# Mixing product of a decoder layer: the second and third block taken together with four seven-multiplication units, and one feed-forward block without sums prepared ahead

## The chip, the core and the metric

The kernel runs on one core of one Trainium2 chip. The metric is the device time of one execution in microseconds (us). Lower is better. The engines of the core have short names in the profile: PE is the matrix engine (PEld its weight loads), DVE the vector engine, ACT the scalar engine, POOL the general engine, and SP the engine that only issues DMA transfers here. Each engine works through its own queue in the order in which the program wrote it. L12 is line 12 of the kernel file.

## What is computed

The kernel computes one decoder layer on 256 tokens of width 2048, all in float32: a half feed-forward, a pair of token mixers (retention and sliding-window attention) with gates, a second half feed-forward, and a gated embedding, each followed by a residual addition and a layer norm. Only these lines matter here:

```python
mixed = (sigmoid(gate_r) * ret_branch + sigmoid(gate_a) * att_branch) @ w_mix_out   # 256x2048 @ 2048x2048
h = layer_norm(alpha * h + mixed, ln_g[1], ln_b[1])
g, u = split(h @ w_ffn2_gu)                                                         # 256x2048 @ 2048x11264
h = layer_norm(alpha * h + 0.5 * (silu(g) * u) @ w_ffn2_down, ln_g[2], ln_b[2])
```

The product with `w_mix_out` is called the mixing product below.

## The kernel before

**A product in three matmuls.** Every operand is kept as two parts, a rounded high part and the low part that is left. One float32 product of a 128x128 piece of the activations and a 128x512 piece of the weights is three matmuls (L393 low by high, L394 high by high, L395 high by low). For each 512 KB of weights, ACT makes the high part (L98) and DVE the low part by a subtraction (L99). `split` (L97) is the helper for both.

**Plain units.** A plain unit, `Single` (L133), is one weight chunk of 256 rows by 512 columns: 1 load, one 128x1024 copy on ACT, one 128x1024 subtraction on DVE, and 12 matmuls for the 256 tokens. A pair of plain units (kind P, with p the pair of row blocks) covers 1024 columns with 24 matmuls. A `Folded` unit (L147, the second of a pair of kind F) is a plain unit whose low part is made by ACT and an adding DMA issued by POOL (L164), with no work for DVE.

**Seven-multiplication units.** `Seven` (L166, kind S) does the work of a plain pair with seven block products instead of eight, so with 21 matmuls. For it DVE makes four sums of weight blocks (L189 to L192, each 128x512) and four low parts (three of 128x1024, one of 128x512), and ACT four high parts. On the activations' side it needs four combinations of blocks, the forms, which `forms_of` (L481) makes once for each group of 512 rows: `whole` adds the two parts (L478), `seven_forms` makes four sums (L466 to L469), and `split` parts the result; DVE waits for ACT's copy in between. `block` (L425) walks through a list of units. It sums the sevens' shared products into four banks of their own (p1, p6, p7, q5), and after the last seven `seven_common` (L497) combines these on DVE (L501 to L504). The eight banks of the accumulator memory are then all in use: four for the block's own sums and four for the sevens.

**Sums prepared ahead.** Kind D, `Prepared` (L209), is a seven unit whose sums and their parts were made much earlier by `sums_ahead` (L238), written to device memory, and are only read back. `AHEAD` (L43) names the blocks of the second feed-forward and the pairs that are treated so. `sums_ahead` is a generator that goes one step whenever `run_side` (L329) is called; the last two entries, those of block 7, are made during the mixing product (L1489).

**The order of the work.** The order on each engine is written out by hand. `plan` lists all units in the order of use. A small planner, `fill` (L279), runs each time a unit is done with: it makes the next loaded units until 45 matmuls' worth (`ahead`) is made in advance, and issues loads until 90 (`far`) is loaded or made, as long as the slots for weights allow it (16 in the mixing product, L1488). A plain unit keeps 2 slots and needs 1 to load and 2 to make; a seven keeps 7 and needs 2 to load and 6 to make. What the planner emits stands in the queues of SP, ACT and DVE at that place of the program, in front of all that is written later.

**The mixing product.** `mixers` (L1136) ends with it. Four blocks of 512 columns (mo0 to mo3) have 8 plain units each. The transposed activations `mix_t` come from `turned` (L1452), which runs as side work: its last four pieces run in the first block. For blocks 0 to 2 the residual block is loaded (L1494), the product is run (`tokens_out`, L405), and DVE adds it to the residual (L1497) and takes the statistics for the norm (L765). The load of the norm's vectors (`load_for_norm`, L775) stands ahead of block 2. In block 3 the last four units are held: `held_out` (L527) first finishes the first 128 tokens, then `Norm` (L652) combines them (L665, which calls L1485), takes the norm, and PE transposes the result (L644, tiles `lnps`) while the other 128 tokens are still computed. At the first unit of block 3 the planner is opened to 26 slots and 136 matmuls (L1504), so it then makes the rest of the mixing weights, two units of the small product `w_pp` and the first six units of the second feed-forward, all ahead of that combination in DVE's queue.

**The second feed-forward.** Eleven blocks of 512 gate and 512 up columns. `gu_units` (L873) gives each block's order: block 7 is PPSDSDSP, with three sevens and two prepared ones; block 8 is PPSSPSSP with four sevens. The first feed-forward has FFSSFSSF.

Of the kernel before, what the change touches and what calls it, by code (L numbers as in the profile page):

```python
# [12 lines left out]
ALU = mybir.AluOpType  # L13
# [9 lines left out]
ALPHA = 2.0**0.25  # L23
LN_EPS = 1e-5
GN_EPS = 1e-5
KD = D // P
# [13 lines left out]

SEVEN = (0, 1, 2, 3)

AHEAD = {1: (4, 5), 2: (4,), 3: (4, 5), 4: (4,), 5: (4, 5), 7: (4, 5)}  # L43
AHEAD_SLOTS = 32

SEVEN_DOWN = (6, 7, 8, 9)
# [9 lines left out]
def layer(ctx: ExitStack, tc: tile.TileContext, io):  # L56
# [348 lines left out]
    def tokens_out(key, n_k, lhs, ps, n=512, before=None):  # L405

        nk = 1024 // n
        sums = [Sum(ps[t][:, :n], n_k) for t in range(2)]
        for c in range(n_k // nk):
            u = take(key + (c,))  # L410
            tokens_chunk(u.chunk, c * nk, lhs, sums, (0, 1), range(nk))
            done(u)
            run_side()
# [11 lines left out]
    def block(name, units, keys, lhs, forms, sums, fold, before=None):  # L425


        sevens = [p for kind, p in units if kind in "SD"]
        if sevens:
            p1, p6, p7, q5 = (Sum(bank(f"{name}s{j}"), len(sevens)) for j in range(4))  # L430
        for j, (kind, p) in enumerate(units):
            if before is not None:
                before(j)
            if kind in "PF":
                for n in range(2):
                    u = take(keys(n, p))
                    tokens_chunk(u.chunk, 2 * p, lhs, [sums[t][n] for t in range(2)], (0, 1))
                    done(u)
                    run_side()
                continue  # L440
            u = take(keys(0, p))
            a11, a12 = (half_of(lhs(2 * p + e), 0) for e in range(2))
            a22 = half_of(lhs(2 * p + 1), 1)
            f5, f6, f7, f3 = forms(p)
            q2, q3, q4 = sums[0][0], sums[0][1], sums[1][0]
            steps = [
                (p1, a11, u.b11), (q2, a12, u.b21), (q3, f3, u.b22), (q5, f5, u.t1),
                (p7, f7, u.t3), (p6, f6, u.t2), (q4, a22, u.t4),
            ]
            if p == sevens[-1]:  # L450
                steps = [steps[j] for j in (0, 3, 5, 4, 1, 2, 6)]
            for to, left, right in steps:
                to.add(left, right)
            done(u)
            run_side()
            if p == sevens[-1]:
                fold(p1.ap, p6.ap, p7.ap, q5.ap)
# [415 lines left out]
    def gu_units(name, j):  # L873
        if j == 0:
            return [("P", p) for p in range(KD // 2)]
        if name == "f2" and j in AHEAD:
            return units_of(*(("PPSDSDSP", SEVEN[:3]) if j % 2 else ("PPSSDSSP", SEVEN)), AHEAD[j])
        order = "PPSSPSSP" if j % 2 == 0 else "PPSPSPSP"
        if name == "f1":
            order = "FFSSFSSF"  # L880
        return units_of(order, SEVEN[: order.count("S")])

# [220 lines left out]
    GATE_UNITS = units_of("PPSSPSSP", (0, 1, 2, 3))  # L1103
    RET_UNITS = units_of("PPPSPSPP", (0, 1))
    gate_keys = lambda b: lambda n, p: ("w_in_f2", 29 + 4 * b + 2 * n, p)
    ret_keys = lambda b: lambda n, p: ("w_ret2", 4 * b + 2 * n, p)

    def plan_mixers():
        plan_tokens(("w_rv", 0), KD)
        for grp in range(8):  # L1110
            plan_features([("w_in_f", grp)], KD)
        for blk in range(1, 4):
            plan_tokens(("w_rv", blk), KD)
        for grp in range(8, 16, 2):
            plan_tokens(("w_in_f2", grp), KD)
        plan_tokens(("w_av",), KD, nk=4)
        for grp in (20, 16, 17, 18, 19):
            plan_features([("w_in_f", grp)], KD)
        for grp in range(21, 29, 2):
            plan_tokens(("w_in_f2", grp), KD)  # L1120
        for b in range(2):
            block_units(GATE_UNITS, gate_keys(b))
        for j in range(0, 8, 2):
            plan_tokens(("w_att2", j), KD // 2)
        for b in range(2):
            block_units(RET_UNITS, ret_keys(b))
        for blk in range(4):
            plan_tokens(("w_mix", blk), KD)

    def later(n, job):  # L1130
        for j in range(n):
# [4 lines left out]
    def mixers(ht, norm, residual, keepers, away):  # L1136
# [291 lines left out]
                act.copy(sig[-1][:, t], ps[t])  # L1428
        assert not side

        def mixer_block(name, units, keys, lhs):

            ps = [banks(name + w) for w in "ab"]
            got = []
            block(name, units, keys, lhs, forms, block_sums(ps, units, KD), lambda *a: got.extend(seven_common(*a)))
            for n in range(2):
                for t in range(2):
                    dve.tensor_tensor(got[n][:, t], got[n][:, t], ps[t][n], ALU.add)
# [47 lines left out]

        lhs = lambda k: of_pairs(mix_t, k)
        slots_for_weights(16)  # L1488
        lazy.append(sums_ahead(ahead[8:], 3, 2))  # L1489
        for blk in range(3):  # L1490
            if blk == 2:
                load_for_norm(1)
            ps = banks(f"mo{blk}")
            y[blk] = load_columns(residual, blk, "mixy")  # L1494
            tokens_out(("w_mix", blk), KD, lhs, ps)
            for t in range(2):
                dve.scalar_tensor_tensor(y[blk][:, t], y[blk][:, t], ALPHA, ps[t], ALU.mult, ALU.add)  # L1497
            block_stats(stats, y, blk)
        y[3] = load_columns(residual, 3, "mixy")
        ps = banks("mo3")  # L1500
        sums = [[Sum(ps[t], KD)] for t in range(2)]
# [316 lines left out]
```

## Time and profile before

| | us |
|---|---|
| median of 3 runs | 2270.05 (2269.02 to 2270.55) |
| the profiled execution | 2269.44 |
| span of its instructions | 2267.3 |

The profile is of one execution. Its span is 2.1 us shorter than the execution's own time. The granted clock of PE was 0.999 over the span. A row of the timeline has the start in us from the span's beginning, the length in us, the engine, the line, the operation, what it writes and reads, the shape, the count of merged instructions, and in brackets the idle time of the engine before it with what ended it. A row of the windows view gives the busy time of each engine in one stretch, with the number of instructions in parentheses.

### The profile page before, as it was taken

What the parts mean: (1) busy time and instruction counts of PE and PEld (TensorE: products, weight loads), DVE (VectorE), ACT (ScalarE), POOL (GpSimd) and SP (SyncE); (2) the same over time, 40 slices, a digit from 0 to 9 for tenths busy, and PEclk for the clock granted to TensorE, in tenths of its full rate; (3) what the DMA queues carried; (4) which work ended last, traced back from release to release, by engine and by line L of the source; (5) the groups of instructions that cost most, each with busy time, mean ns of one, the idle gap of its engine ahead of it and who ended that gap; (6) DMA issues with size and microseconds to landing.
All of it is one profiled execution on the core that took longest, in us unless ns stands there. A gap on an engine that the chain in (4) does not pass through costs nothing.

```text
span 2267.3 us, 29270 instructions
## 1 busy us (share of the span) xinstructions
PE 2258.9 (100%) x10482; PEld 1877.7 (83%) x10482; DVE 1975.9 (87%) x2576; ACT 1272.5 (56%) x1543; POOL 37.1 (2%) x49
## 2 busy tenths in 40 slices
PE   9999999999999999999999999999999999999998
PEld 7888888888888888888778888888888888888887
DVE  7988989999989887888789788689999999889887
ACT  6676776656555444535566454455555565555543
POOL 0000010000000000000000000000000000000000
PEclk9999999999999999999999999999999999999999
DMA  9888898865677878775456568787867766555772
GB/s 316 249 261 252 238 262 243 250 208 186 216 285 261 291 282 289 256 236 183 140 158 225 183 211 293 271 288 247 297 242 250 255 197 218 196 190 209 290 269 73
DMA packets 216889, 536.69 MB, mean 237 GB/s; under 512 B 17052, under 2 KB 21532, under 8 KB 216744
## 3 DMA queue, kind: packets, MB, share of 16 engines
q1 hardware_dynamic: 209000, 511.28, 65.9%
q0 software_dynamic: 5760, 20.97, 5.1%
q10 hardware_dynamic: 1984, 2.58, 0.4%
q8 instruction: 82, 1.34, 0.2%
q14 instruction: 63, 0.52, 0.1%
HBM read 484.43 MB, written 29.36 MB: 227 GB/s over the span
## 4 chain that ended last, share of the span: by engine, by line
PE 78%; DVE 1%; DMA 1%; ACT 0%; issue 0%; ACTq 0%; DVEq 0%
PE f2g L395 3%; PE f2g L393 3%; PE f2g L394 3%; PE rqk L344 3%; PE f2u L393 2%; PE f2u L395 2%; PE f2u L394 2%; PE aqk L344 2%; PE f1d L395 2%; PE f2d L394 2%; PE f2d L395 2%; PE f1d L393 2%; PE f1d L394 2%; PE f2d L393 2%; PE f1e L395 1%; PE f2e L394 1%
## 5 line engine op out<-in xcount | busy, mean ns | idle before, releaser
L99 DVE TENSOR_TENSOR lf_gu<-rf_gu,hf_gu 128x1024 fp32r<-128x1024 f32 (+1 forms) x229 | 271.9, 1210 | 11.1 <-ACT hf_gu L98 10.4
L98 ACT CAST hf_gu<-rf_gu 128x1024 fp32r<-128x1024 f32 (+1 forms) x229 | 232.8, 1041 | 30.2 <-DMA rf_gu<-in_f_gu 29.9
L99 DVE TENSOR_TENSOR lf_down<-rf_down,hf_down 128x1024 fp32r<-128x1024 f32 x150 | 178.8, 1220 | 19.0 <-ACT hf_down L98 18.5
L99 DVE TENSOR_TENSOR lw_in_f<-rw_in_f,hw_in_f 128x1024 fp32r<-128x1024 f32 x140 | 167.5, 1220 | 25.0 <-ACT hw_in_f L98 24.7
L98 ACT CAST hf_down<-rf_down 128x1024 fp32r<-128x1024 f32 x150 | 151.7, 1049 | 50.7 <-DMA rf_down<-in_f_down 18.0
L98 ACT CAST huf_gu<-uf_gu 128x1024 fp32r<-128x1024 f32 x75 | 79.0, 1053 | 147.5 <-DVE uf_gu L190 138.0
L98 ACT CAST hw_in_f<-rw_in_f 128x1024 fp32r<-128x1024 f32 x140 | 140.3, 1050 | 3.2 <-PE rv L394 1.4
L98 ACT CAST hvf_gu<-vf_gu 128x1024 fp32r<-128x1024 f32 x75 | 79.1, 1055 | 31.7 <-DVE vf_gu L192 30.8
L99 DVE TENSOR_TENSOR luf_gu<-uf_gu,huf_gu 128x1024 fp32r<-128x1024 f32 x75 | 91.4, 1219 | 0.0
L99 DVE TENSOR_TENSOR lvf_gu<-vf_gu,hvf_gu 128x1024 fp32r<-128x1024 f32 x75 | 91.4, 1218 | 0.0
L393 PE MATMUL f1g<-hf_gu,xt 128*128 128x512 f32 x232 | 90.6, 390 | 0.2 <-ACT hf_gu L98 0.2
L395 PE MATMUL f1g<-lf_gu,xt 128*128 128x512 f32 x232 | 90.7, 391 | 0.0
L394 PE MATMUL f1g<-hf_gu,xt 128*128 128x512 f32 x232 | 90.4, 390 | 0.0
L393 PE MATMUL f2g<-hf_gu,ht 128*128 128x512 f32 x217 | 84.7, 390 | 0.0
L395 PE MATMUL f2g<-lf_gu,ht 128*128 128x512 f32 x217 | 84.7, 390 | 0.0
L394 PE MATMUL f2g<-hf_gu,ht 128*128 128x512 f32 x217 | 84.5, 390 | 0.0
L994 ACT ACTIVATE eve<-eve 128x1024 f32<-128x1024 f32 x20 | 21.2, 1061 | 100.4 <-DVE eve L993 100.4
L395 PE MATMUL f1u<-lf_gu,xt 128*128 128x512 f32 x192 | 75.0, 390 | 0.7 <-DMA lf_gu<-rf_gu 0.7
L393 PE MATMUL f1u<-hf_gu,xt 128*128 128x512 f32 x192 | 75.7, 394 | 0.0
L394 PE MATMUL f1u<-hf_gu,xt 128*128 128x512 f32 x192 | 74.9, 390 | 0.0
L393 PE MATMUL f2u<-hf_gu,ht 128*128 128x512 f32 x172 | 68.2, 397 | 0.0
L395 PE MATMUL f2u<-lf_gu,ht 128*128 128x512 f32 x172 | 67.1, 390 | 0.0
(1468 smaller groups left out, 6734.7 us busy)
## 6 DMA issues: line engine op xcount, KB each, us to landing
rf_gu<-in_f_gu SPq DMA_DIRECT2D x360, 512.0 KB
rf_down<-in_f_down SPq DMA_DIRECT2D x176, 512.0 KB
rw_in_f<-in_w_in_f SPq DMA_DIRECT2D x148, 512.0 KB
lf_gu<-rf_gu POOLq DMA_DIRECT2D x40, 512.0 KB, 7.0
rw_rv<-in_w_rv SPq DMA_DIRECT2D x32, 512.0 KB
rw_ret<-in_w_ret SPq DMA_DIRECT2D x32, 512.0 KB
rw_mix<-in_w_mix SPq DMA_DIRECT2D x32, 512.0 KB
rw_pg<-in_w_pg SPq DMA_DIRECT2D x32, 512.0 KB
```

Of the source, the lines that this page charges most:

```text
L98: act.copy(dst_hi, src)
L99: (lo_engine or dve).tensor_tensor(dst_lo, src, dst_hi, ALU.subtract)
L344: pe.matmul(ps[f], hi[:, kk, f * P : (f + 1) * P], rhs(k), start=k == 0, stop=k == n_k - 1,)
L393: pe.matmul(o, al, bh, start=first, stop=False)
L394: pe.matmul(o, ah, bh, start=False, stop=False)
L395: pe.matmul(o, ah, bl, start=False, stop=self.left == 0)
L994: act.activation(g, g, AF.Silu)
```

## The change

The mixing product's first block stays plain. The second and third block become one product of 1024 columns with the units PPSSPSSP, so with four sevens (rows 0 to 1023) and four plain pairs; its forms are made from `mix_t` during the first block. The last block stays as it was. Block 7 of the second feed-forward leaves `AHEAD` and takes the order FFSSFSSF, and the `sums_ahead` that ran in the mixing product is gone. The four banks of the sevens are named at the first seven of a block instead of at its beginning. The loads of the two residual blocks and of the norm's vectors move to the fifth and the seventh unit of the joint product.

```diff
-AHEAD = {1: (4, 5), 2: (4,), 3: (4, 5), 4: (4,), 5: (4, 5), 7: (4, 5)}
+AHEAD = {1: (4, 5), 2: (4,), 3: (4, 5), 4: (4,), 5: (4, 5)}
...
         for c in range(n_k // nk):
+            if before is not None and c % 2 == 0:
+                before(c // 2)
             u = take(key + (c,))
...
-        if sevens:
-            p1, p6, p7, q5 = (Sum(bank(f"{name}s{j}"), len(sevens)) for j in range(4))
+        four = []
...
+            if not four:
+                four.extend(Sum(bank(f"{name}s{i}"), len(sevens)) for i in range(4))
+            p1, p6, p7, q5 = four
...
-        if name == "f1":
+        if name == "f1" or j == 7:
             order = "FFSSFSSF"
...
+    MIX_UNITS = units_of("PPSSPSSP", (0, 1, 2, 3))
+    mix_keys = lambda n, p: ("w_mix", 1 + n, p)
...
-        for blk in range(4):
-            plan_tokens(("w_mix", blk), KD)
+        plan_tokens(("w_mix", 0), KD)
+        block_units(MIX_UNITS, mix_keys)
+        plan_tokens(("w_mix", 3), KD)
...
-        lazy.append(sums_ahead(ahead[8:], 3, 2))
-        for blk in range(3):
-            if blk == 2:
+
+        def before_first(j):
+            if j >= 2:
+                made[j - 2] = forms_of(mix_t[2 * j - 4 : 2 * j - 2], f"mof{j}")
+
+        def before_second(j):
+            if j == 4:
+                for blk in (1, 2):
+                    y[blk] = load_columns(residual, blk, "mixy")
+            if j == 6:
                 load_for_norm(1)
-            ps = banks(f"mo{blk}")
-            y[blk] = load_columns(residual, blk, "mixy")
-            tokens_out(("w_mix", blk), KD, lhs, ps)
-            for t in range(2):
-                dve.scalar_tensor_tensor(y[blk][:, t], y[blk][:, t], ALPHA, ps[t], ALU.mult, ALU.add)
-            block_stats(stats, y, blk)
+
+        ps = banks("mo0")
+        y[0] = load_columns(residual, 0, "mixy")
+        tokens_out(("w_mix", 0), KD, lhs, ps, before=before_first)
+        for t in range(2):
+            dve.scalar_tensor_tensor(y[0][:, t], y[0][:, t], ALPHA, ps[t], ALU.mult, ALU.add)
+        block_stats(stats, y, 0)
+        for n, v in enumerate(mixer_block("mos", MIX_UNITS, mix_keys, lhs, before_second)):
+            dve.scalar_tensor_tensor(y[1 + n], y[1 + n], ALPHA, v, ALU.mult, ALU.add)
+            block_stats(stats, y, 1 + n)
```

`mixer_block` (L1431) gets a `before` argument that it hands to `block`. It exists already for the gates and the retention output: after the last unit it adds the block's own four sums to the sevens' result with four DVE operations (L1438).

More of the change, by code (lines that the diff above doesn't have):

```diff
@@ L1429, in mixers, with mixer_block @@
         assert not side
-        def mixer_block(name, units, keys, lhs):
+        def mixer_block(name, units, keys, lhs, before=None):
             ps = [banks(name + w) for w in "ab"]
             got = []
-            block(name, units, keys, lhs, forms, block_sums(ps, units, KD), lambda *a: got.extend(seven_common(*a)))
+            block(name, units, keys, lhs, forms, block_sums(ps, units, KD), lambda *a: got.extend(seven_common(*a)), before)
             for n in range(2):
```

## Prediction

> **What bounds the kernel now.** I read the page first, then the windows view cut at the ends of the four mixing blocks.
>
> ```profile
> PE 2258.9 (100%) x10482; PEld 1877.7 (83%) x10482; DVE 1975.9 (87%) x2576; ACT 1272.5 (56%) x1543; POOL 37.1 (2%) x49
> ```
> ```profile
> 1377.10:1401.10 24.00, 24.00 (x115) 19.89 (x114) 21.97 (x24) 12.71 (x16) 0.00 (x0) 1.00 0.67 238
> 1401.10:1422.90 21.80, 21.80 (x98) 18.07 (x97) 16.44 (x19) 11.00 (x12) 0.00 (x0) 1.00 0.98 341
> 1422.90:1444.60 21.70, 21.70 (x98) 17.97 (x97) 12.80 (x14) 9.01 (x11) 0.00 (x0) 1.00 0.94 371
> 1444.60:1466.30 21.70, 21.70 (x98) 17.93 (x97) 19.95 (x27) 10.08 (x11) 0.00 (x0) 1.00 0.62 202
> ```
>
> PE is busy all the time, DVE (third figure) nearly so in the first and the last mixing block, with room in the second and third. DVE's timeline shows where it waits:
>
> ```profile
> 1390.40 0.69 DVE L99 TENSOR_TENSOR mixt<-mxt,mixt 128x512 fp32r<-128x512 f32 x1 [1.02 <-ACT mixt L98]
> 1391.01 0.68 DVE L257 TENSOR_TENSOR uf_gu<-rf_gu,rf_gu 128x512 f32<-128x512 f32 x1
> ...
> 1400.50 1.37 DVE L1497 SCALAR_TENSOR_TENSOR mixy<-mixy,mo 128x512 f32<-128x512 f32 x2
> ...
> 1402.98 2.34 DVE L99 TENSOR_TENSOR lw_mix<-rw_mix,hw_mix 128x1024 fp32r<-128x1024 f32 x2
> ...
> 1422.26 1.37 DVE L1497 SCALAR_TENSOR_TENSOR mixy<-mixy,mo 128x512 f32<-128x512 f32 x2 [5.32 <-PE mo L395]
> ...
> 1444.02 1.37 DVE L1497 SCALAR_TENSOR_TENSOR mixy<-mixy,mo 128x512 f32<-128x512 f32 x2 [8.01 <-PE mo L395]
> ...
> 1446.50 0.68 DVE L99 TENSOR_TENSOR pt<-praw,pt 128x512 fp32r<-128x512 f32 x1
> 1447.09 4.63 DVE L99 TENSOR_TENSOR lw_mix<-rw_mix,hw_mix 128x1024 fp32r<-128x1024 f32 x4
> ...
> 1457.91 2.54 DVE L99 TENSOR_TENSOR lf_gu<-rf_gu,hf_gu 128x1024 fp32r<-128x1024 f32 x2 [0.52 <-ACT hf_gu L98]
> 1461.38 1.23 DVE L99 TENSOR_TENSOR lf_gu<-rf_gu,hf_gu 128x1024 fp32r<-128x1024 f32 x1 [0.94 <-ACT hf_gu L98]
> 1462.53 0.68 DVE L1485 SCALAR_TENSOR_TENSOR mixy<-mixy,mo 128x512 f32<-128x512 f32 x1
> ```
>
> Three things are read here. Up to 1390.40 DVE is tied to PE: it waits for a transpose. In the middle it idles 5.3 and 8.0 us for PE. At the end it is late: the last block's combination starts at 1462.53, and PE then waits for the norm, as PE's timeline shows:
>
> ```profile
> 1466.27 0.38 PE L644 MATMUL lnps<-ident,mixy 128*128 128x128 f32 x2
> 1466.88 0.44 PE L644 MATMUL lnps<-ident,mixy 128*128 128x128 f32 x2 [0.23 <-DVE mixy L632]
> ```
>
> From combination to second transpose pair is 1466.88 - 1462.53 = 4.35 us. So DVE has no slack at the end of this stage; what lengthens its queue between 1390.40 and 1462.53 beyond its idle time moves the end.
>
> **PE's part of the change.** From 1422.26 to 1444.02, 96 matmuls pass: 21.76 / 96 = 0.227 us each. Four sevens save 4 x 3 = 12 matmuls, 2.7 us. Block 7 goes from five sevens to four and gains 3 matmuls, 0.7 us. The chain of waits, in its rows for the transposes of the feed-forward blocks, shows both lengths already:
>
> ```profile
> 1774.59 0.87 PE f2t L937 x8
> ...
> 1815.61 0.87 PE f2t L937 x8
> ...
> 1857.31 0.87 PE f2t L937 x8
> ```
>
> Block 7 (five sevens) takes 41.02 us, block 8 (four) 41.70. If PE alone counted, the sum would be -2.0 us.
>
> The Trainium skill ("Perfetto Trace Analysis", section "Identifying the Most-Contended Engine") wants PE's headroom judged by weight loads, not by matmul busy time. Loads fill 83% here, so by it 17% would be free and three matmuls could cost nothing (0.7 less below). The trace does not agree that this share can be had: 41.70 against 41.02 is just those three.
>
> **DVE's part, step by step.** The prices are start-to-start times. A block of the gates has the same order, PPSSPSSP:
>
> ```profile
> 1223.86 0.69 DVE L189 TENSOR_TENSOR uw_in_f<-rw_in_f,rw_in_f 128x512 f32<-128x512 f32 x1
> ...
> 1226.60 1.22 DVE L99 TENSOR_TENSOR lw_in_f<-rw_in_f,hw_in_f 128x1024 fp32r<-128x1024 f32 x1
> ...
> 1230.60 0.69 DVE L189 TENSOR_TENSOR uw_in_f<-rw_in_f,rw_in_f 128x512 f32<-128x512 f32 x1
> ...
> 1241.88 0.68 DVE L501 TENSOR_TENSOR evw<-eve,ga1s 128x512 f32<-128x512 f32 x1
> ...
> 1244.59 2.35 DVE L99 TENSOR_TENSOR lw_att<-rw_att,hw_att 128x1024 fp32r<-128x1024 f32 x2
> 1246.86 0.68 DVE L1438 TENSOR_TENSOR eve<-eve,ga1a 128x512 f32<-128x512 f32 x1
> ...
> 1249.25 4.63 DVE L99 TENSOR_TENSOR lw_att<-rw_att,hw_att 128x1024 fp32r<-128x1024 f32 x4
> ```
>
> One seven costs DVE 1230.60 - 1223.86 = 6.74 us, while PE needs 21 x 0.227 = 4.77. The fold (L501 to L504) is 2.7, the four closing sums 2.4, a plain low part 4.63 / 4 less the overlap at its end, 1.14. The forms are priced by the retention's, which also come from two pieces, and the wider combination by L1023:
>
> ```profile
> 1270.11 1.29 DVE L478 TENSOR_TENSOR mrfw<-rett 128x512 f32<-128x512 f32 x2
> ...
> 1274.16 1.23 DVE L99 TENSOR_TENSOR mrfl<-sums,mrfh 128x1024 fp32r<-128x1024 f32 x1 [1.17 <-ACT mrfh L98]
> ```
> ```profile
> L1023 DVE SCALAR_TENSOR_TENSOR f2y<-f2y,eve x2: 1214/1214/1215, 2046.2 to 2148.0; 128x1024 f32<-128x1024 f32 x2
> ```
>
> One group of forms is 1274.16 - 1270.11 + 1.14 = 5.2, of which 1.17 is a wait for ACT's copy that DVE cannot use, its queue being in order.
>
> Now DVE's queue from 1391.0, where it is still tied to PE, in the order the program writes it:
> - in block 0: two groups of forms 10.4, four low parts 4.6, the last mix_t piece 0.6: 1406.6. (The prepared sums that stood here from 1391.01 on are gone: twice four sums, 1226.60 - 1223.86 = 2.74, and two low parts, by the gates' prices 10.0 us.)
> - combination and statistics of block 0, 1402.98 - 1400.50 = 2.5: 1409.1. PE ends that block at 1401.1 (one block of 21.8 before 1422.26 + 0.68, the second half's sum), so DVE, coming to it at 1406.6, waits for nothing.
> - two sevens 13.5, two low parts 2.3, two sevens 13.5, two low parts 2.3, two of block 3 2.3, fold 2.7, two more 2.3: 1448.0.
> - four closing sums 2.4, two combinations 2 x 1.14, four statistics 4 x 0.6: 1455.1.
> - the tail as before: from 1446.50 to 1462.53 is 16.0, less the two waits for loads 1.5, which the delay covers: 14.5. The combination starts at 1469.6.
>
> That is 7.1 us later than 1462.53, and PE's second transpose pair comes 7.1 later with it, at 1474.0. Is PE itself there by then? Its first seven could start at 1401.1 + 4 x 2.72 = 1412.0, and the low part it needs first is ready 3.9 us after the seven's start on DVE, at 1413.0. The second seven is ready so at 1409.1 + 6.74 + 3.9 = 1419.7, when PE has been free since 1417.5: a wait of about 2 us. The fourth starts on DVE at 1431.6 and is complete at 1438.4, and PE needs its last low part two products after a nominal start of 1434: 2 to 3 us more. So PE ends the joint product near 1447 and block 3 near 1469, 5 us ahead of the transposes. **The 2.7 us saved are spent waiting for DVE.** Behind each waiting matmul stands all of PE's queue.
>
> Costed at nothing: ACT, busy 42.8 of 89.2 us in the four rows of the windows (it gets one copy for each new low part and none of the sums, so it stays behind DVE's load); the loads of residual blocks 1 and 2 and of the norm's vectors, seven transfers on SP that move later, past weight loads, and are read only after 1448, when the closing sums begin; the banks, since block 0's two are free at about 1408 and the sevens' banks are first written after 1412 (4 us of cover; beyond it a wait would add one to one); the loads removed, which lower the transfers' share (0.98 and 0.94 in the middle rows). DVE in block 7: four folded units save 4 x 1.14, two prepared ones become sevens, and the block stays under block 8's load, which PE passes without a wait.
>
> The adding DMAs of block 7's folded units are not seen in this feed-forward. In the first one there are 40:
>
> ```profile
> lf_gu<-rf_gu POOLq DMA_DIRECT2D x40, 512.0 KB, 7.0
> ```
> ```profile
> PE f1u L395 <- DMA lf_gu<-rf_gu: 0.7, 1, 0.7
> ```
>
> One of 40 held PE for 0.7 us. For four, I take 0, with 0 and 2.8 as ends.
>
> **Sum.** 2269.44 + 7.1 + 0.7 = 2277.2. The profiled execution lies 0.6 under the median of the runs shown, so 2277.5 for a median; 0.3% slower.
>
> The Trainium skill ("VectorE: DVE Perf Modes", section "The DRAIN you can't avoid") says that a DVE operation does not start until the one before has left the pipe. Then each of some 90 operations would cost its full length, 0.08 us more, and the result would be about 2284.5. The trace does not agree: four of 1.22 us take 4.63 together, not 4.9.
>
> **Rivals.**
> 1. Not slower: PE stays the bound, because DVE's queue is shorter than I count, by forms that fall into its waits before 1391 or by sevens made in the idle 13 us (it would need to end 7 us sooner). Then -2.0, and the 0.4 us wait at the norm goes too: 2267.0. For it speaks that DVE idles 13.3 us in blocks 1 and 2. Against it: that idle time and the 10.0 us removed are 23, and the forms (10.4), the sevens' surplus 4 x (6.74 - 2.28) = 17.8, fold and closing sums (5.1) are 33, in a stage 2.7 us shorter. Chance 0.15.
> 2. Slower still: the weights come late. With 16 slots the planner asks for the third seven only when the second is done with, 24 matmuls (5.4 us) ahead, where a plain unit was asked for 84 ahead. One transfer took 4.64 us to land in the chain of waits:
>
> ```profile
> 1455.57 4.64 DMA rf_gu<-in_f_gu
> ```
> If the load were issued only then, near 1424, DVE would wait until about 1429 for its two chunks instead of starting at 1425: 4 us more, 2281.5. Against it, SP runs ahead of that place:
> ```profile
> 1365.95 0.37 SPq L112 DMA_DIRECT2D rw_mix<-in_w_mix  x1
> ```
> This is the first chunk of block 1, which the planner asks for after the first unit of block 0, at about 1380: 14 us early. Chance 0.18.
> 3. The change does not do in block 7 what it says: the folded units' DMAs hold PE as in the one case above, each 0.7: 2280. Chance 0.04.
> 4. The rule on the pipe, 2284.5: 0.02.
>
> **How the numbers follow.** The forecast (DVE's queue ends last, 2273 to 2280) has 0.61. A measurement of this kernel can tell about 0.2%, 4.5 us. Slower by more than that, above 2274.6: most of the forecast (0.52) and rivals 2 to 4, 0.76. Within it: the rest of the forecast and most of rival 1, 0.22. Faster by over 0.2% would need 4.5 us, twice what PE can gain: 0.02. The range 2269.5 to 2282.5 leaves out rival 1's point and the far end of rivals 2 to 4.
>
> **What would show it.** Right: DVE without a wait for PE between 1391 and 1445; PE waiting for DVE's low parts at the second and fourth seven; the transposes of the norm 6 to 8 us later and waiting 4 to 5; block 7 at 41.7 us with no wait. Wrong: DVE idle before PE in the joint product, or SP or loads ending DVE's waits there, or a stall at a folded unit.

## The result and the profile after

The changed kernel takes 2278.53 us (median of 5 runs, 2277.07 to 2281.71), the kernel before 2270.05: a ratio of 1.004 with the interval 1.0027 to 1.0053. It is slower by 0.4%; the forecast was 2277.5. The profiled execution is the one of 2278.53 us, its span 2276.7.

The page's first row of the changed kernel, for the shares:

```profile
PE 2260.5 (99%) x10473; PEld 1875.6 (82%) x10473; DVE 1996.7 (88%) x2610; ACT 1283.7 (56%) x1556; POOL 40.6 (2%) x53
```

It tells little; the stage does. PE has less to do in the mixing product and still ends it later. First the windows of the changed kernel, cut where its three parts begin and end on PE (columns as before: length, then PE, PEld, DVE, ACT, POOL, and the granted clock behind POOL):

```profile
1378.00:1402.00 24.00, 24.00 (x115) 19.86 (x114) 21.17 (x28) 7.09 (x9) 0.00 (x0) 1.00 0.27 88
1402.00:1447.40 45.40, 42.20 (x182) 33.30 (x181) 43.77 (x54) 28.20 (x32) 0.00 (x0) 1.00 0.76 269
1447.40:1469.14 21.74, 21.74 (x97) 17.82 (x95) 21.67 (x24) 11.78 (x12) 0.00 (x0) 1.00 0.81 256
1469.14:1478.40 9.26, 5.01 (x18) 3.68 (x18) 8.05 (x18) 1.85 (x5) 0.00 (x0) 0.82 0.25 94
```

DVE is busy 43.77 of the 45.40 us of the joint product (second row) and all through block 3 (third row). PE stands idle for 3.2 us in the joint product and for over 4 us in the last row. Behind the transpose that it waits for up to 1391.28, DVE waits only twice before 1469.7 us, both times in the forms, for ACT's copy (from the view of waits: total us, times, longest):

```profile
DVE mof2l L99 <- ACT mof2h L98: 1.2, 1, 1.2
DVE mof3l L99 <- ACT mof3h L98: 1.1, 1, 1.1
```

DVE's timeline at the corners of that chain (form of the rows as before; the helpers' lines stand four lower):

```profile
1391.89 1.28 DVE L482 TENSOR_TENSOR mof2w<-mixt 128x512 f32<-128x512 f32 x2
...
1407.35 1.28 DVE L1512 SCALAR_TENSOR_TENSOR mixy<-mixy,mo 128x512 f32<-128x512 f32 x2
...
1409.74 0.67 DVE L189 TENSOR_TENSOR uw_mix<-rw_mix,rw_mix 128x512 f32<-128x512 f32 x1
...
1443.27 0.68 DVE L505 TENSOR_TENSOR evw<-eve,moss 128x512 f32<-128x512 f32 x1
...
1448.24 0.68 DVE L1445 TENSOR_TENSOR eve<-eve,mosa 128x512 f32<-128x512 f32 x1
...
1455.54 0.68 DVE L99 TENSOR_TENSOR pt<-praw,pt 128x512 fp32r<-128x512 f32 x1
1456.13 4.62 DVE L99 TENSOR_TENSOR lw_mix<-rw_mix,hw_mix 128x1024 fp32r<-128x1024 f32 x4
...
1469.75 0.68 DVE L1492 SCALAR_TENSOR_TENSOR mixy<-mixy,mo 128x512 f32<-128x512 f32 x1
```

And what PE waits for, in its waits; in the kernel before, the wait at `lnps` was 0.23 us, none stood at `moss`, and the one at `f1u` was 0.7 us:

```profile
PE lnps L648 <- DVE mixy L636: 4.2, 2, 3.9
PE moss L395 <- DVE lw_mix L99: 2.3, 3, 1.6
PE f1u L395 <- DMA lf_gu<-rf_gu: 1.3, 2, 1.0
PE moss L395 <- DVE luw_mix L99: 0.8, 1, 0.8
PE moss L395 <- DVE lvw_mix L99: 0.2, 1, 0.2
```

The waits at `moss` (the sevens' shared banks) are new, and the one at `lnps` (the norm's transposes) has grown from 0.2 to 4.2 us. No folded unit of block 7 holds PE: `f1u` is the first feed-forward.

One thing was not foreseen. PE's timeline right behind the norm's wait, and the clock there by windows:

```profile
1473.19 0.56 PE L648 MATMUL lnps<-ident,mixy 128*128 128x128 f32 x2 [3.89 <-DVE mixy L636]
1474.11 0.69 PE L648 MATMUL lnps<-ident,mixy 128*128 128x128 f32 x2 [0.35 <-DVE mixy L636]
...
1475.03 0.63 PE L394 MATMUL pp<-hw_pp,pt 128*128 128x512 f32 x1
1475.45 0.63 PE L395 MATMUL pp<-lw_pp,pt 128*128 128x512 f32 x1
```
```profile
1475.00:1477.00 2.00, 2.00 (x7) 1.54 (x5) 1.97 (x5) 0.62 (x2) 0.00 (x0) 0.55 0.00 0
1477.00:1480.00 3.00, 3.00 (x17) 2.48 (x16) 0.50 (x1) 0.96 (x2) 0.00 (x0) 1.00 0.00 0
```

The granted clock falls to half for 3.4 us, from 1473.37 to 1476.78, and the matmuls of `pp` start 0.42 us apart instead of 0.23.

**Where the 9.09 us between the two profiled executions lie.** A stage is measured from the first matmul of the mixing product to the first transpose of the second feed-forward:

```profile
1377.31 0.39 PE L393 MATMUL mo<-hw_mix,mixt 128*128 128x512 f32 x1
...
1527.63 1.03 PE L937 MATMUL f2t<-ident,f2v 128*128 128x128 f32 x8
```
```profile
1378.19 0.39 PE L393 MATMUL mo<-hw_mix,mixt 128*128 128x512 f32 x1
...
1536.10 1.03 PE L941 MATMUL f2t<-ident,f2v 128*128 128x128 f32 x8
```

The first pair of rows is the kernel before (150.32 us), the second the changed one (157.91): 7.59 longer. Of these, 6.35 are there at the norm's second transposes (1474.11 - 1466.88, less the 0.88 by which the stage began later), and 1.24 come behind them, with the low clock (from there to the stage's end 61.99 us instead of 60.75). The 0.88 is from ahead of the change: 0.80 of it in the first feed-forward. Block 7 is 0.68 longer, the end of the kernel 0.27, and the span's surroundings are 0.33 shorter: 0.88 + 7.59 + 0.68 + 0.27 - 0.33 = 9.09.

### The profile page after: what moved, and what is told of

Its sections match the earlier page's. It is cut to its first block, busy times and chain, and to the rows that moved or that the text cites. A ratio compares the mean times of both kernels' runs of the same rounds, so it can differ in the third digit from the quotient of the medians.

```text
span 2276.7 us, 29268 instructions
## 1 busy us (share of the span) xinstructions
PE 2260.5 (99%) x10473; PEld 1875.6 (82%) x10473; DVE 1996.7 (88%) x2610; ACT 1283.7 (56%) x1556; POOL 40.6 (2%) x53
## 4 chain that ended last, share of the span: by engine, by line
PE 76%; DVE 3%; issue 1%; DMA 1%; ACT 0%; ACTq 0%; DVEq 0%
PE f2g L393 3%; PE f2g L395 3%; PE f2g L394 3%; PE rqk L344 3%; PE f2u L393 2%; PE f2u L394 2%; PE f2u L395 2%; PE aqk L344 2%; PE f2d L395 2%; PE f1d L394 2%; PE f2d L393 2%; PE f1d L395 2%; PE f1d L393 2%; PE f2d L394 2%; PE f2e L395 1%; PE f2e L394 1%
## 5 line engine op out<-in xcount | busy, mean ns | idle before, releaser
L164 POOL DMA_DIRECT2D lf_gu<-rf_gu x44 | 38.2, 868 | 1766.6 <-DVE lf_gu L99 1386.6
```

What stands on the lines that cost most here:

```text
L164: pool.dma_start(c.lo, c.raw, accum_op=ALU.add)
```

## The experiments

The theory: DVE's queue from 1391 on ends last; the last block's combination waits for it, and PE for the combination. Rivals: the weights come late; PE's own side of the change costs something; each seven, not the queue's end, costs the time. All runs are in one table. A ratio is to the kernel before as measured again beside that run (2269.87 to 2270.18 us). Line numbers in the rows of the experiments can differ by a few from those of the changed kernel. The stage is the one just measured, and so does not hold what an execution loses ahead of it; the wait is PE's idle time at the norm's first two groups of transposes; the last column is the granted clock right behind them.

| kernel | median us | ratio to before (interval) | stage us | wait us | clock |
|---|---|---|---|---|---|
| before | 2270.05 | | 150.32 | 0.2 | 1.0 |
| changed | 2278.53 | 1.004 (1.0027 to 1.0053) | 157.91 | 4.2 | 0.55 |
| b7_only | 2270.30 | 1.0002 (0.9994 to 1.0011) | 149.89 | 0 | 1.0 |
| four_only | 2269.53, one run | | 149.89 | 0 | 1.0 |
| slots22 | 2278.44 | 1.0038 (1.0024 to 1.0052) | 157.79 | 4.1 | 0.5 |
| no_forms | 2272.35 | 1.0011 (1.0001 to 1.002) | 152.31 | 3.1 | 0.52 |
| keep_busy | 2277.45 | 1.0033 (1.002 to 1.0045) | 156.70 | 0.7 | 1.0 |
| fold_front | 2278.13 | 1.0039 (1.0024 to 1.0055) | 157.02 | 3.0 | 0.5 |
| fold_tail | 2284.24 | 1.0062 (1.0048 to 1.0076) | 164.36 | 4.8 | 0.5 |
| fold_both | 2284.72 | 1.0067 (1.0054 to 1.0079) | 164.88 | 4.5 | 0.5 |
| three_sevens | 2274.35 | 1.0017 (1.0008 to 1.0026) | 153.53 | 3.3 | 0.5 |
| two_sevens | 2273.45 | 1.0012 (1.0003 to 1.002) | 152.98 | 2.4 | 0.50 |
| late_f2 | 2282.44 | 1.0048 (1.0033 to 1.0064) | 161.15 | 0.9 | 1.0 |
| two_early | 2268.30 | 0.9992 (0.9983 to 1.0001) | 148.56 | 0 | 1.0 |

### Block 7 and the banks alone

b7_only is the kernel before with the edits of block 7 only:

```diff
-AHEAD = {1: (4, 5), 2: (4,), 3: (4, 5), 4: (4,), 5: (4, 5), 7: (4, 5)}
+AHEAD = {1: (4, 5), 2: (4,), 3: (4, 5), 4: (4,), 5: (4, 5)}
...
-        if name == "f1":
+        if name == "f1" or j == 7:
...
-        lazy.append(sums_ahead(ahead[8:], 3, 2))
```

> The kernel before with block 7 of the second feed-forward as FFSSFSSF and no prepared sums in the mixing product, which stays plain. My theory (DVE's queue ends last in the mixing stage; block 7 costs its three matmuls): block 7 takes 41.7 us instead of 41.0, and the 0.4 us wait at the norm's transposes does not grow; 2270.0 to 2270.8, so within 0.2% of before. Rival (block 7's adding DMAs hold PE): 2272 or more, with PE waits on a DMA in that block.

four_only is the kernel before with the four banks named at the first seven, as in the change:

```diff
-        if sevens:
-            p1, p6, p7, q5 = (Sum(bank(f"{name}s{j}"), len(sevens)) for j in range(4))
+        four = []
...
+            if not four:
+                four.extend(Sum(bank(f"{name}s{i}"), len(sevens)) for i in range(4))
+            p1, p6, p7, q5 = four
```

> The kernel before with only one part of the change: the sevens' four banks are named at the first seven of a block, not at its beginning. My theory (a bank is taken at its first use, so this moves nothing): 2269.0 to 2271.0, the first feed-forward with its usual waits of 0.5 to 2 us for adding DMAs. Rival (it changes which banks the blocks wait for): new PE waits on DVE or ACT at the sevens of the feed-forward blocks, or a span longer by over 3 us.

In b7_only the chain of waits has block 7 between these rows, 41.70 us as forecast, and the median does not move:

```profile
1774.05 0.87 PE f2t L937 x8
1815.75 0.87 PE f2t L937 x8
```

Both kernels have the stage at 149.89 us, 0.43 under the kernel before. For b7_only one would put that down to the sums that are gone; four_only still makes them and shows the same. So the 0.4 us at the norm in the profile of the kernel before (a wait of 0.23 and what it delays) most likely differs from execution to execution, which no run here tests, and the two edits cost nothing in the stage.

### Are the weights late?

slots22 is the changed kernel with 22 slots instead of 16 in the mixing product:

```diff
-        slots_for_weights(16)
+        slots_for_weights(22)
```

> The changed kernel with 22 slots for weights in the mixing product instead of 16, so the planner asks for the sevens' chunks earlier. My theory (DVE's work, not the loads, sets the pace): combination of the last block within 0.3 us of 1469.75, total 2278 to 2279. Rival (weights come late under 16 slots): DVE idles less, 2274 to 2276.

PE's wait at the norm is that of the changed kernel, and so are its waits in the joint product:

```profile
PE lnps L648 <- DVE mixy L636: 4.1, 2, 3.9
```

More slots change nothing, and DVE waits for no load between 1391.28 and 1469.75 us in the changed kernel. The rival is refuted.

### A shorter queue, and a clock that is kept up

no_forms leaves the two groups of forms of the mixing product out (the sevens take the retention output's):

```diff
-            if j >= 2:
-                made[j - 2] = forms_of(mix_t[2 * j - 4 : 2 * j - 2], f"mof{j}")
+            made[1] = made[0]
```

> The changed kernel, but the forms of the mixing product's activations are left out: the sevens multiply by the retention's forms, which are there already. DVE is spared 10.2 us before the first seven. My theory (a chain of DVE work up to the last block's combination): DVE then reaches block 0's combination early and waits there for PE, so only 5.9 us are gained: combination near 1463.8, PE's wait at the norm about 3 us or less and no reduced clock behind it; 2270.5 to 2272. Rival (the weights' arrival sets the pace): 2277 or more. Rival (PE's own work sets it): no change, 2278.

keep_busy puts work for PE in front of the norm's first transposes, 34 transposes of the identity whose results are not used:

```diff
+            if (self.i, t, c) == (1, 0, 0):
+                spare = bank("lnw")
+                for _ in range(34):
+                    pe.transpose(spare[:, :P], ident, ident)
             if c == 0:
```

> The changed kernel with 34 extra 128x128 transposes on PE (about 3.7 us) directly ahead of the norm's first transposes, where PE waited 4.0 us for DVE; DVE's work is the same. My theory (the low clock of 0.5 for 3.4 us behind the wait is a price of PE's idleness): the granted clock stays 1.0 there, first real transposes at the same time, and 1.2 to 1.6 us are gained: 2276.9 to 2277.4. Rival (the low clock has another cause, or costs nothing because PE is ahead of DVE anyway): 2278.5 or a little more.

Without the forms PE waits for no low part in the joint product, and the stage is 5.6 us shorter, though the forms are 10.3 us of DVE's time. Most of the rest goes into waits in block 0, where DVE now comes too early: 4.0 us from 1391 on, of them 2.4 for PE at the end of that block, as was expected. From there to the combination DVE waits for nothing and takes 62.4 us, as in the changed kernel. From DVE's timeline, and PE's waits:

```profile
1400.53 1.37 DVE L1511 SCALAR_TENSOR_TENSOR mixy<-mixy,mo 128x512 f32<-128x512 f32 x2 [2.44 <-PE mo L395]
```
```profile
PE lnps L648 <- DVE mixy L636: 3.1, 2, 2.7
```

The time is just above the range that was expected: the clock fell after a wait of only 2.7 us, which was not expected (0.52 on the mean from 1468 to 1471).

In keep_busy the clock stays up, with the same delay on DVE; the same window as in the changed kernel:

```profile
1475.00:1477.00 2.00, 2.00 (x11) 1.66 (x10) 1.97 (x5) 0.88 (x3) 0.00 (x0) 1.00 0.01 4
```

Its stage is 1.21 us shorter than the changed kernel's, and from the norm's second transposes to the stage's end it takes 60.78 us, as the kernel before does (60.75; changed 61.99). The medians differ by 1.1 with overlapping intervals, so it is the trace that carries this. The 1.24 us behind the transposes is the clock.

### Low parts moved from DVE to adding DMAs

fold_front makes the first four plain units of the joint product folded ones (a new kind G, both units of a pair `Folded`); fold_tail does so with the last four units of block 3 and three of the first six units of the second feed-forward; fold_both does both.

```diff
-    MIX_UNITS = units_of("PPSSPSSP", (0, 1, 2, 3))
+    MIX_UNITS = units_of("GGSSPSSP", (0, 1, 2, 3))
...
+            elif kind == "G":
+                plan.extend(Folded(keys(n, p)) for n in range(2))
```
```diff
-        plan_tokens(("w_mix", 3), KD)
+        plan.extend((Single if c < 4 else Folded)(("w_mix", 3, c)) for c in range(KD // 2))
...
-            return [("P", p) for p in range(KD // 2)]
+            return [("F" if name == "f2" and p < 3 else "P", p) for p in range(KD // 2)]
```

> The changed kernel, with all four units of the joint product's first two plain pairs folded: their low parts come from ACT and adding DMAs, so DVE is spared 4 x 1.14 = 4.6 us ahead of the first seven, PE's work is the same. My theory (DVE's queue is one chain up to the last block's combination): everything behind is 4.6 us earlier, the waits for the sevens' low parts go (4.0 us), but the wait at the norm stays near 3.5 us with the low clock behind it; 2273.5 to 2275. Rival (the sevens' own waits for DVE are the whole loss): the norm's wait goes too, 2271 or less. Rival (adding DMAs come late): PE waits on DMAs at the folded units, 2277 or more.

> The changed kernel, with the last four units of the last mixing block and three of the first six units of the next feed-forward folded: DVE is spared 7 x 1.14 = 8.0 us, all behind the joint product. My theory: the waits for the sevens' low parts stay (4.0 us), the combination comes 8 us earlier, near 1461.8, so the wait at the norm (4.05 + 0.6) and the low clock behind it (1.2) go and PE is the bound there; 2272 to 2273.2. Rival (the loads of these units hold DVE or PE, not DVE's work): 2275 or more.

> Both of the former: DVE spared 12.5 us. My theory: neither the sevens nor the norm wait for DVE any more, the 12 matmuls saved in the joint product come through, block 7 keeps its 3 more: 2267.2 to 2268.8, about 0.1% under the kernel before. Rival (the two reliefs overlap, or adding DMAs take the place of DVE): 2270 or more, with PE waits for a DMA or for DVE in the mixing stage.

All three miss the theory's number, and the rivals (the adding DMAs, and the loads beside them, come late) are what happened; fold_both has the waits of both. In fold_front the waits for DVE's low parts are gone and PE waits for the DMAs instead, with the low clock behind that wait too. Against the stage's start the combination comes only 0.7 us earlier, not 4.6: DVE, with less to do, waits longer for ACT's copies, 2.1 us for one of them. From PE's waits:

```profile
PE mosa L395 <- DMA lw_mix<-rw_mix: 2.3, 2, 2.0
```
In fold_tail four such DMAs stand among the loads of the second feed-forward and take 12 us. PE waits for them in block 3, and the slots they hold back delay the loads: SP, which issues the loads, waits 8.2 us for one of these DMAs, ACT waits for the loads, 5.0 and 4.3 us, and DVE for ACT. From its waits (SPq is SP's queue), its DMA issues (KB each, median us from issue to landing) and DVE's timeline:

```profile
PE mo L395 <- DMA lw_mix<-rw_mix: 3.8, 3, 1.7
SPq L112 <- DMA lw_mix<-rw_mix: 8.2, 1, 8.2
```
```profile
lw_mix<-rw_mix POOLq DMA_DIRECT2D x4, 512.0 KB, 12.0
```
```profile
1470.48 1.23 DVE L99 TENSOR_TENSOR lf_gu<-rf_gu,hf_gu 128x1024 fp32r<-128x1024 f32 x1 [6.11 <-ACT hf_gu L98]
```

DVE had less to do and ended later, at 1474.6. That DVE's queue is too long does not make every way of shortening it a gain. Whether folded units issued earlier would gain was not tried.

### Fewer sevens, less ahead of the combination

```diff
-    MIX_UNITS = units_of("PPSSPSSP", (0, 1, 2, 3))
+    MIX_UNITS = units_of("PPSPSPSP", (0, 1, 2))
```
```diff
-    MIX_UNITS = units_of("PPSSPSSP", (0, 1, 2, 3))
+    MIX_UNITS = units_of("PPPSPSPP", (0, 1))
...
-            if j >= 2:
+            if j == 2:
```

The first is three_sevens, the second two_sevens (which needs only the first group of forms).

> The joint product has three sevens (PPSPSPSP on rows 0 to 767), each followed by a plain pair; both groups of forms are made. DVE's queue gets shorter than in the changed kernel by one seven less two plain low parts, 4.4 us; PE has 3 matmuls more (0.68 us). Theory: no seven stands behind another on DVE, so PE waits under 1 us in the joint product; the combination comes 4.4 us earlier, near 1465.4, the norm's transposes wait under 1.5 us, the clock stays at 1.0, and the time is 2278.5 - 4.4 - 1.2 = 2272.9 or, where PE is then the bound, lower: 2270 to 2273.5. Rival (the clock falls behind this kernel's norm whatever the wait): 1.2 us more. Rival (the waits of PE in the joint product carry the loss, not DVE's end): they go here, about 4 us, and the norm still waits 4: 2274 to 2276.

> The joint product has two sevens (PPPSPSPP on rows 0 to 511) instead of four, and only one group of forms is made. DVE's queue gets shorter than in the changed kernel by two sevens less four plain low parts, 2 x (6.7 - 2.28) = 8.8 us, and one group of forms, 5.2: 14.0 us. PE then needs 6 matmuls fewer than the kernel before in the mixing product (1.36 us) and 3 more in block 7 (0.68). Theory (the stage was lost because DVE's queue ended last): no wait of PE for a low part in the joint product, no wait of more than 0.3 us at the norm's transposes, granted clock 1.0 behind them, and 2269.4 - 1.36 - 0.4 + 0.68 = 2268.3 (2267.8 to 2269.6 with the first feed-forward's shifts). Rival (each seven waits for itself on DVE, however long the queue): one wait of 2 us at the second seven, and 2269.5 to 2271. Rival (a block of this form costs something on PE, such as the change of banks): over 2271 without a wait of PE for DVE.

late_f2 keeps four sevens, but lets the planner make less ahead at block 3:

```diff
-        slots_for_weights(26, 136, 160)
+        slots_for_weights(26, 100, 160)
```

> The changed kernel, but at block 3 the planner may make 100 matmuls ahead instead of 136, so the low parts of three units of the second feed-forward (3 x 1.14 = 3.4 us on DVE) come behind the norm's first part instead of ahead of the last combination. Nothing else on DVE or PE changes its order. Theory: the combination comes 3.4 us earlier, near 1466.3, the transposes wait about 0.7 instead of 4.05 us, the clock stays at 1.0, and the time is 2278.5 - 3.4 - 1.2 = 2273.9 (2273 to 2275.5). Rival (the low parts moved are then late for the second feed-forward): PE waits there and the gain is under 2 us: 2276.5 to 2279. Rival (the clock falls after any such stage): 2275.1.

The times of all three lie above the ranges that were expected; the traces show why.

**three_sevens.** Counted from the start of the stage, the combination comes 4.4 us earlier than in the changed kernel, as expected (1466.87 - 1379.70 = 87.17 against 1469.75 - 1378.19 = 91.56). But PE, which no longer waits for low parts, is earlier too, so it still waits 3.3 us at the norm, and the clock falls.

**two_sevens.** DVE should have been 14 us shorter; the combination came 5.3 earlier. DVE's timeline shows the rest:

```profile
1432.01 0.69 DVE L505 TENSOR_TENSOR evw<-eve,moss 128x512 f32<-128x512 f32 x1 [3.57 <-PE moss L395]
...
1442.14 0.69 DVE L1445 TENSOR_TENSOR eve<-eve,mosa 128x512 f32<-128x512 f32 x1 [2.79 <-PE mosa L395]
...
1444.86 0.69 DVE L1445 TENSOR_TENSOR evw<-evw,mosa 128x512 f32<-128x512 f32 x1 [1.35 <-PE mosa L395]
...
1451.05 0.67 DVE L99 TENSOR_TENSOR pt<-praw,pt 128x512 fp32r<-128x512 f32 x1
...
1465.71 0.68 DVE L1492 SCALAR_TENSOR_TENSOR mixy<-mixy,mo 128x512 f32<-128x512 f32 x1
```

PE waits at no seven in this kernel, so it is not each seven that costs the time. DVE idles 7.7 us for PE, and then, behind PE's last matmul of the joint product, has two closing sums, both combinations and all four statistics to do: 1451.05 - 1444.86 = 6.2 us. In the kernel before only one block's combination and statistics came there, 1446.50 - 1444.02 = 2.5. So there is a second bound, 3.7 us longer than in the kernel before, that no shorter queue takes away: PE's end of the joint product, this work, and the tail. In no_forms DVE comes to this work at 1441.45, just as PE ends the joint product (its last matmul starts at 1441.58), so there the two bounds nearly meet.

**late_f2.** The combination comes 3.4 us earlier against the stage's start, as expected (1467.30 - 1379.16 = 88.14), the wait at the norm falls to 0.9, the clock stays up: that DVE's queue sets the norm is shown from this side as well. But the three low parts moved behind the norm bring ACT's copies with them, and PE waits for those:

```profile
PE f2u L393 <- ACT hf_gu L98: 4.6, 2, 2.3
```

The stage is 3.2 us longer than the changed kernel's. What stood ahead of the combination had its reason to stand there.

### The closing work done ahead

two_early is two_sevens with the residual combined right behind the fold, in DVE's idle time, and the block's own sums added to it as their banks are done; block 9 gets block 7's order as well.

```diff
-        if name == "f1" or j == 7:
+        if name == "f1" or j in (7, 9):
...
-            if j == 4:
+            if j == 2:
                 for blk in (1, 2):
                     y[blk] = load_columns(residual, blk, "mixy")
...
-        for n, v in enumerate(mixer_block("mos", MIX_UNITS, mix_keys, lhs, before_second)):
-            dve.scalar_tensor_tensor(y[1 + n], y[1 + n], ALPHA, v, ALU.mult, ALU.add)
+        ps = [banks("mos" + w) for w in "ab"]
+
+        def fold(*a):
+            for n, v in enumerate(seven_common(*a)):
+                dve.scalar_tensor_tensor(y[1 + n], y[1 + n], ALPHA, v, ALU.mult, ALU.add)
+
+        block("mos", MIX_UNITS, mix_keys, lhs, forms, block_sums(ps, MIX_UNITS, KD), fold, before_second)
+        for n in range(2):
+            for t in range(2):
+                dve.tensor_tensor(y[1 + n][:, t], y[1 + n][:, t], ps[t][n], ALU.add)
             block_stats(stats, y, 1 + n)
```

> The joint product has two sevens as before in the run with two sevens, but the residual blocks are combined with the sevens' result right behind the fold, and the block's own four sums are added to them as each pair of banks is done; block 9 of the second feed-forward takes the order FFSSFSSF as well (four sevens instead of three, 3 matmuls fewer). In the run with two sevens DVE idled 7.7 us for PE in the joint product and had 6.2 us of work (1444.86 to 1451.05) behind PE's last matmul of it, where the kernel before had 2.5 behind each block. Theory (what holds the norm's transposes is DVE's work behind PE's end of the joint product, and it is 3.7 us longer for a pair of blocks than for one): the work behind PE's end is 2.5 us, the combination comes 3.7 us earlier, the transposes wait under 0.4 us, the clock stays at 1.0; 2269.4 - 1.36 - 0.4 + 0.68 - 0.68 = 2267.7 and with the first feed-forward's shift of 0 to 2.4 us at most 2270.1; the stage from the first matmul of the mixing product to the norm's second group is 1.7 us shorter than before, block 9 is 41.7 us. Rival (the loads of the second feed-forward, asked for at block 3, end the wait, not that work): DVE waits for ACT's copies ahead of the combination, the transposes wait 1.5 to 2.5 us as with two sevens, 2271.5 to 2273. Rival (block 9 stalls at a folded unit): 0.5 to 2 us more, shown at that block.

```profile
1433.12 1.22 DVE L1518 SCALAR_TENSOR_TENSOR mixy<-mixy,eve 128x1024 f32<-128x1024 f32 x1
...
1443.26 0.69 DVE L1523 TENSOR_TENSOR mixy<-mixy,mosa 128x512 f32<-128x512 f32 x1 [0.16 <-PE mosa L395]
...
1445.73 0.68 DVE L99 TENSOR_TENSOR pt<-praw,pt 128x512 fp32r<-128x512 f32 x1
...
1461.30 0.68 DVE L1492 SCALAR_TENSOR_TENSOR mixy<-mixy,mo 128x512 f32<-128x512 f32 x1
```

From the last pair of sums to the tail is now 2.5 us (1445.73 - 1443.26), and against the stage's start the tail begins 3.7 us earlier than in two_sevens, as expected. The combination comes only 2.8 us earlier: the tail is 0.9 us longer (15.6 against 14.7), with 1.0 us of waits for ACT's copies in place of 0.4. PE waits neither in the joint product nor at the norm, the clock stays at 1.0, and the stage is 148.56 us, 1.76 shorter than before and 1.33 shorter than without the norm's wait (149.89): the six matmuls saved, 1.36. Block 9 gained two thirds of what was expected, 41.91 us instead of 42.38, not 41.70. The missing 0.2 us is in its folded units: a weight load of PE waits there for an adding DMA, and the matmuls at it start 0.30 and 0.34 us apart instead of 0.23:

```profile
PEld f2u L395 <- DMA lf_gu<-rf_gu: 0.3, 1, 0.3
```

The median is 2268.30 against 2269.87 in the same runs, and the interval, 0.9983 to 1.0001, just takes in no difference: that the whole kernel is faster is not shown, only that the stage of the profiled execution is.

## Why the prediction was right

**The sum** was 2277.2 for the profiled execution, which took 2278.53. By steps, each counted from the same point, the first operation of the forms:

| DVE's step | forecast us | measured us |
|---|---|---|
| forms, four low parts, `mix_t` | 15.6 | 15.5 |
| block 0's combination and statistics | 2.5 | 2.4 |
| four sevens, low parts, to the fold | 33.9 | 33.5 |
| fold and two low parts | 5.0 | 5.0 |
| closing sums, combinations, statistics | 7.1 | 7.3 |
| tail | 14.5 | 14.2 |
| all | 78.6 | 77.9 |

The measured ones are the differences of the rows quoted above. The prices from the gates' block and from the retention's forms hold within 2%; the wider combination was priced 0.1 us too low (1.24 us, not 1.14). So 7.1 us became 6.35. This is the step that carries the forecast. three_sevens and late_f2 move the combination by just the time that they take off DVE's queue (4.4 and 3.4 us), no_forms by what is left of it behind DVE's waits in block 0 (5.9 of 10.3).

**PE's waits** were forecast at 2 us at the second seven (1.6), 2 to 3 at the fourth (1.3 in three pieces), about 5 at the transposes (4.2). A wait of 0.3 at the first seven was not named. The 2.7 us of saved matmuls went there, as was said: PE's waits in the joint product are 3.3 us together.

**Block 7** is 41.70 us, as read from block 8, and none of its folded units held PE. The Trainium skill's rule on weight loads as headroom ("Perfetto Trace Analysis", section "Identifying the Most-Contended Engine") is not borne out: with loads at 82% of the span three matmuls more cost 0.68 us, the whole of their time. Of the DVE pipe the Trainium skill ("VectorE: DVE Perf Modes", section "The DRAIN you can't avoid") says not only that the next operation waits until the pipe is empty, but also that one which is not held starts earlier; the prediction left the second half out. The trace agrees with the second half: four subtractions that are 1.22 us long alone again take 4.62 together, and the chain came out shorter than the sum, not longer.

**What was not in the sum.** The low clock, 1.24 us, shown by keep_busy. What is lost ahead of the stage, 0.88, of it 0.80 in the first feed-forward: the instructions of its first 400 us stand in the same order in both kernels, its end shifts by -0.1 to 2.4 us from profile to profile of all these kernels against the one before, and PE's waits for adding DMAs in it are 0.3 to 1.9 us; what sets this was not found. With the 0.75 that DVE was quicker, the end's 0.27 and the 0.33 around the span, 1.24 + 0.88 - 0.75 + 0.27 - 0.33 = 1.3, the difference between sum and measurement. That it is no larger is in part luck: the terms that were left out would have been 2.1 us, had DVE not been quicker than priced.

**The rivals.** Late weights: refuted by slots22. Folded units holding PE in block 7: not seen. PE staying the bound: it did not, but the condition given for it was wrong. That DVE "would need to end 7 us sooner" only brings DVE back to where it was, while PE for its -2.0 us would itself be 2.7 us earlier, so nearly 10 us are needed: in no_forms the combination comes 5.9 us sooner and PE still waits 3.1 us. What the prediction did not name, though it has it as a term, is that the closing work of two blocks falls at one place. With four sevens this was hidden, since DVE came to it later than PE; with two it is the bound.

## What to carry to other kernels

Before work is taken off a full engine and put on another that is nearly full, write out the second engine's queue, from the last point where it waits for the first engine to the point for which the first waits; prices from an equal block of the same trace gave that sum to 1%. Then look for the second bound behind it: when two blocks become one, what each did at its end now stands in one piece behind the last matmul, and what of it can be done ahead of that should be. A wait that appears on PE may cost more than its length, by the clock that falls behind it.

## What the runs showed of the hardware

The half clock came after shorter waits than expected. It followed PE waits of 3.9 us (changed kernel), 2.7 us (no_forms) and 1.9 us (two_sevens), and lasted 3.4 us; in fold_tail and fold_both, behind waits of 4.6 and 4.2 us, it lasted twice as long, 6.8 us. Here are two_sevens' waits, and the windows up to the fall of the clock and behind it:

```profile
PE lnps L648 <- DVE mixy L636: 2.4, 2, 1.9
```

```profile
1467.57:1470.98 3.41, 1.35 (x7) 1.02 (x8) 3.23 (x10) 1.37 (x5) 0.00 (x0) 1.00 0.58 213
1470.98:1474.39 3.41, 3.41 (x9) 2.65 (x9) 2.44 (x5) 0.37 (x1) 0.00 (x0) 0.50 0.00 0
```

The clock changes at fixed places that do not start with the wait. In fold_front it falls twice, at 1410.70 and at 1472.14, each time for 3.41 us, and the two falls are 61.44 us apart, which is 18 times 3.413; in the other traces, too, the changes of the clock lie a whole number of such lengths apart:

```profile
1410.70:1414.11 3.41, 3.41 (x9) 2.66 (x9) 3.41 (x5) 0.98 (x2) 0.00 (x0) 0.50 1.03 237
1472.14:1475.55 3.41, 3.08 (x9) 2.30 (x10) 3.34 (x8) 1.56 (x4) 0.00 (x0) 0.50 0.01 4
```

In late_f2 a wait of 2.3 us brought the fall and a second one of the same length did not. Cut at those places, PE is busy 1.08 us in the window that ends with the fall, and 1.65 us in the one with most of the second wait, whose rest lies in the next; the clock stays at 1.0 behind it:

```profile
1481.84:1485.25 3.41, 1.08 (x7) 0.74 (x6) 1.17 (x3) 2.75 (x6) 0.00 (x0) 1.00 0.97 312
1488.67:1492.08 3.41, 1.65 (x10) 1.16 (x8) 1.94 (x4) 1.69 (x3) 0.00 (x0) 1.00 1.04 398
```

So the length of the wait alone does not decide; how much of it falls into one such window fits what is seen. Where a clock of 1.0 falls in or behind the mixing stage of these kernels, PE was busy at most 1.40 us of the window before, and no window there with 1.65 us or more was followed by a fall. That this share sets the fall is not shown: no run moved a wait against the windows and left the rest as it was.

The Trainium skill ("TensorE: Matmul & The Clock Gate", section "What's actually happening") tells of an activity window of 3413 ns that runs free of the kernel, and in "HAM oscillation — how this bites in real kernels" gives gaps over about 3.4 us as the ones to avoid. The length and the places of the low stretches agree with that window; the limit of 3.4 us does not agree with the falls after 1.9, 2.3 and 2.7 us.

An adding DMA of 512 KB has no fixed price. Its median from issue to landing is 6.9 us over the 44 of the two feed-forwards of the changed kernel, 5.0 over the four of fold_front's joint product, and 12.0 over the four of the mixing weights in fold_tail, where they stand among weight loads; no run tested what sets it.

```profile
lf_gu<-rf_gu POOLq DMA_DIRECT2D x44, 512.0 KB, 6.9
```
